# A two-network transformer kernel: the ALiBi bias from GpSimd to VectorE, and the norms' steps at other places among the products

## The chip, the cores and the metric

The kernel runs on one core of a Trainium2 chip. The metric is device time in microseconds (us) of one execution, from the first to the last instruction on the device, together with the little that lies around them. A kernel is run several times and the median counts.

## The reference, cut to what matters

Two networks run one after the other on 256 positions of 1024 features, in float32. The first has two layers, each an attention, a SwiGLU feed-forward and a gated input (PLE); the second has a convolution and pooling mixer, a feed-forward with a short convolution, an attention, and another such feed-forward.

```python
for i in range(DEPTH):                       # first network, two layers
    hn = rmsnorm(h, norm_mix[i])
    mix = diff_attention(hn, ...) if i % 2 == 0 else neighborhood_attention(hn, ...)
    h = h + mix
    h = h + swiglu(rmsnorm(h, norm_ffn[i]), ffn_w_gate[i], ffn_w_up[i], ffn_w_down[i])
    gate = jax.nn.sigmoid(rmsnorm(h, norm_ple[i]) @ ple_w_gate[i])
    h = h + gate * (p[i] @ ple_w_proj[i])
return rmsnorm(h, norm_final)
# second network: h += even_mixer(norm(h)); h += conv_ffn(norm(h))
#                 h += odd_mixer(norm(h));  h += conv_ffn(norm(h)); final norm
# in diff_attention, for each of 8 heads:
    dist = jnp.abs(qpos[:, None] - kpos[None, :]).astype(jnp.float32)
    bias = -slopes[:, None, None] * dist
    s = einsum('mbhqd,mbhkd->mbhqk', qblk, k) * scale + bias
# rmsnorm: x * rsqrt(mean(x * x) + eps) * g, a mean over the 1024 features
```

## The kernel before

Activations lie feature by feature: 8 tiles of 128 features (partitions) by 256 positions, handled as 4 banks of two tiles. The weights are streamed from HBM in chunks of 128 x 1024 by DMAs that SyncE issues, into a stage of 5 buffers. Each chunk is split into a rounded high part (`w_hi`, ScalarE, L96) and the rest (`w_lo`, VectorE, L97), into a pool of 8 buffers. Every product is done as three matmuls of a 128 x 128 weight with 256 columns (`mm3`, all at L220): high with high, high with low, low with high. The activations are split in the same manner (`u_hi` on ScalarE, L282, `u_lo` on VectorE, L284).

The order of the matmuls is written out by hand. The program counts steps: after every 12 matmuls (4 `mm3`) `tick()` moves a clock on and runs what is due, so `at(delay, f)` puts f among the products that follow, and splits of later chunks are paid out there too. The order on the other engines comes out of the order of emission through a scheduler.

A norm is folded into the products: they use `u`, the activations with the gain alone, and the results are multiplied by `R`, the factors 1/rms laid out over all partitions, when they are read from PSUM (the accumulator memory of TensorE). The factors take two steps, which `rstd_soon(n, a, b)` puts at two ticks. Step a (`rstd_a`) adds up the squares on TensorE (`ps_ss`, a matmul with ones that reads `half`, the VectorE sum at L291), scales on VectorE (L306), and takes the power on GpSimd (POOL, L307). Step b (`rstd_b`) spreads the result with two transposes on TensorE (`ps_r`, L323) and a copy on ScalarE (`R`, L325). `first_pairs(u, late=2)` lets four column tiles of weights (96 matmuls) start over the first 6 of the 8 feature tiles and takes the last 2, whose bank comes last, afterwards.

In an attention `qkv_group` computes q and k of a group (`ps_g`, 48 matmuls each), reads them with the factors, and then v (`ps_v`, 48 matmuls); the scores (`ps_S`) and the softmax run at ticks that the table `AT` lists. In the first group a loop waits with reading until R is emitted:

```python
while g == 0 and not hasattr(n, "R"):
    tick()
```

At the start of the program, SP loads x and the weights; GpSimd makes `dist` (the distances, 128 x 512) and, in `small_constants` at tick 9, multiplies it by the slopes of 8 heads: eight `tensor_scalar` of 128 x 512 (L573, `bias`). The same GpSimd queue holds the power of the first norm behind them. In PLE the four banks of the gate's products are read and turned into the new h in the order 0, 1 (both after the product of bank 2), 2, 3. In the feed-forwards a pair is 48 matmuls; the first two pairs come from `first_pairs`, and a product of the result (`acc`, reading `m` of L805) begins after the fourth.

Of the kernel before, what the change touches and what calls it, by code (L numbers as in the profile page):

```python
# [13 lines left out]
OP = mybir.AluOpType  # L14
# [19 lines left out]


AT = {
    "da": {"scores": (3, 9), "then": (6, 8, 12), "last": ((2, 5), (5, 7, 10)), 0: (6, 10)},
    "na": {"scores": (3, 9), "then": (6, 8), "last": ((2, 5), (5, 7)), 0: (6, 10)},
    "od": {"scores": (3, 9), "then": (6, 8), "last": ((2, 5), (5, 7)), 0: (12, 15), 1: (6, 9)},
}  # L40


# [81 lines left out]
def network(ctx: ExitStack, tc: tile.TileContext, x_t, p_t, cols, b_v, na_bias, t5_bias, w_mats, out):  # L124
# [88 lines left out]
    causal = off  # L213
    tri = const.tile([128, 128], F32, name="tri")

    def col(name, i):
        return ct[:, COL[name] + i:COL[name] + i + 1]

# [13 lines left out]
    def at(delay, f):  # L232
        clock[1] += 1
        due.append((clock[0] + delay, clock[1], f))
# [96 lines left out]
    def release():  # L331
        W.hold = False

    def rstd_soon(n, a=7, b=9):
        at(4, release)
        at(a, lambda: rstd_a(n))
        at(b, lambda: rstd_b(n))

    def bc2(r):
        return r[:, None, :].to_broadcast([128, 2, S])  # L340
# [127 lines left out]
    def qkv_group(n, g, kind, bv, steps):  # L468
        q = work.tile([128, 2, S], F32, tag="q", bufs=1, name="q")
        k = work.tile([128, 2, S], F32, tag="k", bufs=1, name="k")  # L470

        def parts(x, tag):
            hi = work.tile([128, 2, S], F32R, tag=tag + "h", name=tag + "_hi")
            lo = work.tile([128, 2, S], F32R, tag=tag + "l", name=tag + "_lo")
            nc.scalar.activation(hi, x, AF.Copy)
            nc.vector.tensor_sub(lo, x, hi.bitcast(F32))
            return x, hi, lo

        v = work.tile([128, 2, S], F32, tag="v", name="v")
        u = n.u  # L480
        ps_k = None
        if g == 0 and kind != "da":
            ps, ps_k = first_pairs(u)
        else:
            ps = pair(u)
            if g == 0:
                ps_k = pair(u)
        while g == 0 and not hasattr(n, "R"):
            tick()
        if kind == "na":  # L490
            t = work.tile([128, 2, S], F32, tag="qb", bufs=1, name="qb")
            nc.vector.tensor_mul(t, ps, bc2(n.R))
            for i in range(2):
                nc.scalar.activation(q[:, i, :], t[:, i, :], AF.Identity, bias=b_q8[:, 2 * g + i:2 * g + i + 1],
                                     scale=0.125)
        else:
            nc.vector.scalar_tensor_tensor(q, ps, 0.125, bc2(n.R), op0=OP.mult, op1=OP.mult)
        q = parts(q, "q")
        ps = ps_k or pair(u)
        if kind == "na":  # L500
            t = work.tile([128, 2, S], F32, tag="qb", bufs=1, name="kb")
            nc.vector.tensor_mul(t, ps, bc2(n.R))
            for i in range(2):
                nc.scalar.activation(k[:, i, :], t[:, i, :], AF.Identity, bias=col("b_k", 2 * g + i), scale=1.0)
        else:
            nc.vector.tensor_mul(k, ps, bc2(n.R))
        k = parts(k, "k")
        steps(q, k, v)
        if kind == "od" and g == 0:
            z = small.tile([128, 2, 8], F32, tag="zf", bufs=1, name="zf")  # L510
            pz = [psum.tile([128, 264], F32, tag=f"acc{2 + t}", name="pz") for t in range(2)]
            kk = 0
            for n_k in (3, 3, 2):
                hi, lo = W.take(n_k * 264)
                for i in range(n_k):
                    for t in range(2):
                        for a, b in ((0, hi), (1, hi), (0, lo)):
                            mm(pz[t], u[a][:, kk, t * 128:(t + 1) * 128], b[:, i * 264:(i + 1) * 264],
                               kk == 0 and (a, b) == (0, hi), kk == 7 and b is lo)
                    kk += 1  # L520
                    if kk % 2 == 0:
                        tick()
            for t in range(2):
                nc.scalar.activation(v[:, t, :], pz[t][:, :256], AF.Copy, scale=n.rstd[:, t:t + 1])
                nc.vector.scalar_tensor_tensor(z[:, t, :], pz[t][:, 256:264], n.rstd[:, t:t + 1],
                                               ct[:, COL["b_f"]:COL["b_f"] + 8], op0=OP.mult, op1=OP.add)
            fox_prepare(z, extra)
            return
        pv = psum.tile([128, 2, S], F32, tag="acc3", name="ps_v")
        for half in range(2):  # L530
            hi, lo = W.take(1024)
            for i in range(4):
                kk = 4 * half + i
                for t in range(2):
                    for c, (a, b) in enumerate(((0, hi), (1, hi), (0, lo))):
                        mm(pv[:, t, :], u[a][:, kk, t * 128:(t + 1) * 128], b[:, i * 256:(i + 1) * 256],
                           kk == 0 and t == 0 and c == 0, kk == 7 and c == 2, skip_group_check=True)
                if i % 2 == 1:
                    tick()
        for t in range(2):  # L540
# [26 lines left out]
    g_fm = const.tile([128, 8], F32, name="g_fm")  # L567

    def small_constants():

        nc.vector.scalar_tensor_tensor(dist, dist, -1.0, dist, op0=OP.mult, op1=OP.max)
        for hd in range(8):
            nc.gpsimd.tensor_scalar(da_tiles[hd // 4][:, hd % 4], dist, -2.0 ** (-8.0 * (hd + 1) / 8), None, op0=OP.mult)  # L573
        nc.vector.tensor_scalar(tri, off[:, :128], 0.0, None, op0=OP.is_ge)
        for g, w in enumerate(POOL_WINDOWS):
            nc.vector.tensor_scalar(rcnt[:, g, :], rcnt[:, g, :], float(w), None, op0=OP.min)
        nc.vector.reciprocal(rcnt, rcnt)
# [12 lines left out]
        nc.vector.tensor_mul(g_fm, ct[:, COL["norm_final"]:COL["norm_final"] + 8], ct[:, COL["mix2"]:COL["mix2"] + 8])  # L590
# [104 lines left out]
    def attention(n, kind, gain_next):  # L695
# [35 lines left out]
        nn, done = next_norm(gain_next)  # L731
        acc.last([(o[0][:, j, :], o[1][:, j, :]) for j in range(8 - N_LAST_ATT, 8)], 8 - N_LAST_ATT, done)
        assert not due
        rstd_soon(nn)
        return nn


# [121 lines left out]
    def ple(n, l, gain_next, after, final=False):  # L859
# [14 lines left out]
        for b in range(4):  # L874
            if b == 0:
                pgs = first_pairs(n.u, between=proj)
                held = [(i, pps[i], pgs[i]) for i in range(2)]
            elif b > 1:
                proj(b)
                held.append((b, pps[b], pair(n.u, *(("m", 2) if b == 2 else ("g", 2)))))  # L880
            if b < 2:
                continue
            for i, pp, pg in held:
                z = work.tile([128, 2, S], F32, tag="a", bufs=3, name="z")
                nc.vector.tensor_mul(z, pg, bc2(n.R))
# [13 lines left out]

    n = Norm()  # L900
    W.split(4, lambda b: norm_bank(n, b, h[:, 2 * b:2 * b + 2, :], lambda t: col("norm_mix", t)))
    W.split()
    for b in range(4):
        stats_bank(n, b, h[:, 2 * b:2 * b + 2, :])
        W.split()
    for _ in range(N_HI - 8):
        W.split()
    at(9, small_constants)
    ug = [const.tile([128, 2 + S], F32, name=f"ug{i}") for i in range(3)]
    for t in ug:  # L910
        nc.gpsimd.memset(t[:, 0:2], 0.0)
# [2 lines left out]
    for l in range(2):  # L914
        n = attention(n, ("da", "na")[l], lambda t, l=l: col("norm_ffn", 8 * l + t))
        n = ffn(n, swiglu_mid, lambda t, l=l: col("norm_ple", 8 * l + t))
        rstd_soon(n)
        if l == 0:
            def after(nn):
                rstd_soon(nn)  # L920
# [11 lines left out]
            nc.vector.scalar_tensor_tensor(h[:, t, :], h[:, t, :], col("norm_final", t), r,  # L932
                                           op0=OP.mult, op1=OP.mult)

    rstd_soon(n)
    at(8, scale_h)


    y = split_act()
# [64 lines left out]
    plan = [(pool_out, 0), (pool_out, 2), (gc_val, 0), (gc_val, 1), (gate_b, 0), (gc_val, 2), (gc_val, 3), (gate_b, 2)]  # L1004
    for i, (f, a) in enumerate(plan):
        if i == 0:
            first = first_pairs(n.u, tags[:2])
        ps = first[i] if i < 2 else pair(n.u, tags[i], 2 if tags[i] == "g" else 1)
        waiting.append((f, ps, a))
        if hasattr(n, "R"):  # L1010
# [13 lines left out]
    nn, done = next_norm(lambda t: col("ffn2", t))  # L1024
    acc.last([y_k(2), y_k(3)], 6, done)
    n = nn
    rstd_soon(n)
    load_t5()
    n = ffn(n, conv_mid(0), lambda t: col("mix2", 8 + t))
    rstd_soon(n)  # L1030
# [178 lines left out]
```

## Time and profile before

| | |
|---|---|
| Median of 3 runs | 1254.99 us (1249.63 to 1255.4) |
| The profiled execution: its own time | 1255.7 us |
| Its span, first to last instruction | 1253.9 us |
| Mean granted TensorE clock | 0.991 |
| TensorE busy (PE) | 1219.8 us, 97% |
| VectorE busy (DVE) | 930.2 us, 74% |
| ScalarE busy (ACT) | 693.4 us, 55% |
| GpSimd busy (POOL) | 56.5 us, 5% |
| SyncE's weight queue | 50.2% of the 16 DMA engines' span |

The page gives each engine's busy time as a share of the span. In rows of the timeline the first number is the start in us from the start of the span, the second the time to the end of the instruction (or of several alike, then with xN), and in brackets stands how long the engine idled before it and what ended that. A matmul overlaps the next, so its step is the distance of two starts.

### The profile page before, as it was taken

The page shows a single profiled execution, that of the slowest core. Times are in us where ns is not written, and L with a number is a line of the kernel's source. Part 1 is how long each engine was busy: PE and PEld are TensorE (multiplying, and loading weights), DVE is VectorE, ACT ScalarE, POOL GpSimd, SP SyncE. Part 2 cuts the span into 40 slices and gives each one's busy share as a digit, 9 for nine tenths or more (in the row PEclk, how much of TensorE's full clock was granted, in tenths as well). Part 3 has the DMA queues.
Part 4 walks back from the last instruction along what each step waited for, and adds up shares of the span by engine and source line. Part 5 has one row for each costly group of instructions (what it writes and reads, how often), then busy time and mean ns, then how long its engine had stood idle before and what let it go on. Part 6 is the DMA issues. An engine that isn't in the chain of part 4 may idle for free.

```text
span 1253.9 us, 25715 instructions
## 1 busy us (share of the span) xinstructions
PE 1219.8 (97%) x10448; PEld 1199.9 (96%) x10448; DVE 930.2 (74%) x1700; ACT 693.4 (55%) x1178; POOL 56.5 (5%) x64
## 2 busy tenths in 40 slices
PE   4999999999999999999999999999999999999997
PEld 4999999999999899999998999999999899999996
DVE  5876766666888767666678978777787876977773
ACT  4776644444667655454457555555455665545543
POOL 6011000000001000000000000000000000000000
PEclk9999999999999999999999999999999999999998
DMA  7554556555557436555544465555545333655530
GB/s 265 186 169 152 174 202 203 196 194 168 202 174 204 175 135 211 193 202 195 180 157 160 160 227 183 200 188 186 185 154 203 122 131 135 218 185 185 187 117 35
DMA packets 62935, 222.46 MB, mean 177 GB/s; under 512 B 7264, under 2 KB 7776, under 8 KB 62688
## 3 DMA queue, kind: packets, MB, share of 16 engines
q1 hardware_dynamic: 60768, 214.52, 50.2%
q0 software_dynamic: 1616, 5.77, 1.9%
q8 instruction: 82, 1.34, 0.4%
q10 hardware_dynamic: 432, 0.53, 0.1%
q14 instruction: 37, 0.30, 0.1%
HBM read 219.74 MB, written 1.05 MB: 176 GB/s over the span
## 4 chain that ended last, share of the span: by engine, by line
PE 86%; DVE 6%; issue 3%; POOL 2%; ACT 2%; DMA 1%; POOLq 0%; DVEq 0%; ACTq 0%; SPq 0%
PE ps_g L220 50%; PE acc L220 26%; PE ps_v L220 4%; DVE w_lo L97 2%; PE ps_V L220 2%; POOL bias L573 1%; PE ps_S L220 1%; PE ps_t L433 1%; POOL rstd L307 1%; ACT w_hi L96 1%; PE ps_p L220 1%; ACT sc L463 0%; PE pz L220 0%; DMA stage<-w_ev_out 0%; PE ps_ss L220 0%
## 5 line engine op out<-in xcount | busy, mean ns | idle before, releaser
L96 ACT ACTIVATE w_hi<-stage 128x1024 fp32r<-128x1024 f32 (+2 forms) x413 | 426.6, 1040 | 411.4 <-PE ps_g L220 174.4
L97 DVE TENSOR_TENSOR w_lo<-stage,w_hi 128x1024 fp32r<-128x1024 f32 (+2 forms) x413 | 493.1, 1201 | 194.8 <-ACT w_hi L96 191.3
L220 PE MATMUL ps_g<-u_hi,w_hi 128*128 128x256 f32 x2048 | 576.5, 281 | 10.2 <-ACT w_hi L96 7.0
L220 PE MATMUL ps_g<-u_hi,w_lo 128*128 128x256 f32 x2048 | 571.1, 279 | 1.2 <-DVE w_lo L97 1.2
L220 PE MATMUL ps_g<-u_lo,w_hi 128*128 128x256 f32 x2048 | 571.3, 279 | 0.7 <-DVE u_lo L284 0.6
L220 PEld LDWEIGHTS ps_g<-u_hi,w_hi 128*128 128x128 f32 x2048 | 386.2, 189 | 14.5 <-ACT w_hi L96 7.0
L220 PEld LDWEIGHTS ps_g<-u_hi,w_lo 128*128 128x128 f32 x2048 | 386.3, 189 | 1.4 <-DVE w_lo L97 1.4
L220 PEld LDWEIGHTS ps_g<-u_lo,w_hi 128*128 128x128 f32 x2048 | 385.8, 188 | 1.1 <-DVE u_lo L284 1.1
L220 PE MATMUL acc<-m,w_hi 128*128 128x256 f32 x1408 | 246.5, 278 | 0.1
L220 PEld LDWEIGHTS acc<-m,w_hi 128*128 128x128 f32 x1408 | 213.6, 188 | 0.4 <-DVE m L805 0.3
L220 PE MATMUL acc<-m,w_lo 128*128 128x256 f32 x704 | 195.4, 278 | 0.0
L220 PEld LDWEIGHTS acc<-m,w_lo 128*128 128x128 f32 x704 | 132.2, 188 | 0.0
L220 PE MATMUL acc<-u_hi,w_hi 128*128 128x256 f32 x256 | 73.0, 285 | 0.0
L220 PE MATMUL acc<-u_hi,w_lo 128*128 128x256 f32 x256 | 71.4, 279 | 0.0
L220 PE MATMUL acc<-u_lo,w_hi 128*128 128x256 f32 x256 | 71.3, 279 | 0.0
L463 ACT ACTIVATE sc<-sc,st 128x256 f32<-128x256 f32 (+1 forms) x96 | 46.0, 481 | 31.4 <-DVE st L461 31.3
L307 POOL TENSOR_TENSOR rstd<-rstd,mhalf 128x2 f32<-128x2 f32 x11 | 15.7, 1426 | 1036.6 <-DVE rstd L306 1036.6
L220 PE MATMUL ps_v<-w_hi,u_hi 128*128 128x256 f32 x176 | 52.5, 298 | 0.0
L220 PE MATMUL ps_v<-w_hi,u_lo 128*128 128x256 f32 x176 | 50.3, 286 | 0.0
L220 PE MATMUL ps_v<-w_lo,u_hi 128*128 128x256 f32 x176 | 50.3, 286 | 0.0
L220 PEld LDWEIGHTS acc<-u_hi,w_hi 128*128 128x128 f32 x256 | 48.0, 188 | 1.5 <-issue 1.1
L220 PEld LDWEIGHTS acc<-u_hi,w_lo 128*128 128x128 f32 x256 | 48.1, 188 | 0.0
(191 smaller groups left out, 1226.8 us busy)
## 6 DMA issues: line engine op xcount, KB each, us to landing
stage<-w_gu SPq DMA_DIRECT2D x88, 512.0 KB, 4.2
stage<-w_in SPq DMA_DIRECT2D x88, 512.0 KB, 4.2
stage<-w_down SPq DMA_DIRECT2D x44, 512.0 KB, 4.3
stage<-w_out SPq DMA_DIRECT2D x44, 512.0 KB, 4.3
stage<-w_na_qkv SPq DMA_DIRECT2D x24, 512.0 KB, 4.2
stage<-w_da_qkv SPq DMA_DIRECT2D x23, 512.0 KB, 4.3
stage<-w_od_in SPq DMA_DIRECT2D x22, 512.0 KB, 3.5
stage<-w_gate SPq DMA_DIRECT2D x16, 512.0 KB, 3.2
```

The source lines that it names most:

```text
L96: self.nc.scalar.activation(hi[:, s], t[:, s], AF.Copy)
L97: self.nc.vector.tensor_sub(lo[:, s], t[:, s], hi[:, s].bitcast(F32))
L220: nc.tensor.matmul(o, a, b, start=start, stop=stop, **kw)
L307: nc.gpsimd.tensor_tensor(n.rstd, st[:, 2:4], mhalf, op=OP.pow)
L433: nc.tensor.transpose(ps[:, o:o + 128], a[:, qt, kk * 128:(kk + 1) * 128], ident)
L463: nc.scalar.activation(sc[:, i, :widths[i]], sc[:, i, :widths[i]], AF.Exp, bias=st[:, 2 + i:3 + i], accum_out=st[:, 4 + i:5 + i])
L573: nc.gpsimd.tensor_scalar(da_tiles[hd // 4][:, hd % 4], dist, -2.0 ** (-8.0 * (hd + 1) / 8), None, op0=OP.mult)
```

## The change

- The eight ALiBi products go to VectorE. Three of them, with the small constants `tri`, `dist` and `rcnt`, are emitted at the start of the program, one at tick 9, four at tick 22.
- In `qkv_group` the loop that waited for R goes. In a first group q and k stay in PSUM, the v products follow at once, and `read()` between them reads q and k as soon as R is there. `AT` lets the first group's scores start a tick earlier (od: two).
- `rstd_soon` puts step b at tick 10 instead of 9; in the conv feed-forwards the steps are at 8 and 11 instead of 7 and 9, ahead of PLE at 5 and 7, ahead of the even mixer at 7 and 11, with `scale_h` (the rescaling of h there) at 13 instead of 8. The neighbourhood attention (na) and the even mixer (ev) take the last 4 feature tiles late instead of 2.
- PLE handles banks 0 and 1 right behind the first pairs.
- The second weight chunk is split in two halves.

```diff
-    "da": {..., 0: (6, 10)},
+    "da": {..., 0: (5, 9)},
...
+    def da_bias(heads):
+
+        for hd in heads:
+            nc.vector.tensor_scalar(da_tiles[hd // 4][:, hd % 4], dist, -2.0 ** (-8.0 * (hd + 1) / 8), None, op0=OP.mult)
+
+    nc.vector.tensor_scalar(tri, off[:, :128], 0.0, None, op0=OP.is_ge)
+    nc.vector.scalar_tensor_tensor(dist, dist, -1.0, dist, op0=OP.mult, op1=OP.max)
+    da_bias(range(3))
...
-    def rstd_soon(n, a=7, b=9):
+    def rstd_soon(n, a=7, b=10):
...
-        while g == 0 and not hasattr(n, "R"):
-            tick()
...
+        waiting = []
+        if g:
+            qs = evict_q(pair(u))
+            steps(qs, evict_k(pair(u)), v)
         else:
-            nc.vector.tensor_mul(k, ps, bc2(n.R))
-        k = parts(k, "k")
-        steps(q, k, v)
+            waiting += first_pairs(u, late=4 if kind == "na" else 2) if kind != "da" else [pair(u), pair(u)]
+
+        def read():
+            if waiting and hasattr(n, "R"):
+                qs = evict_q(waiting[0])
+                steps(qs, evict_k(waiting[1]), v)
+                waiting.clear()
...
                 if i % 2 == 1:
                     tick()
+                    read()
...
-        for hd in range(8):
-            nc.gpsimd.tensor_scalar(da_tiles[hd // 4][:, hd % 4], dist, -2.0 ** (-8.0 * (hd + 1) / 8), None, op0=OP.mult)
+        da_bias([3])
...
-        rstd_soon(nn)
+        rstd_soon(nn, *((8, 11) if kind == "od" else (7, 10)))
...
                 pgs = first_pairs(n.u, between=proj)
+                continue
+            if b == 1:
                 held = [(i, pps[i], pgs[i]) for i in range(2)]
-            elif b > 1:
+            else:
                 proj(b)
                 held.append((b, pps[b], pair(n.u, *(("m", 2) if b == 2 else ("g", 2)))))
-            if b < 2:
-                continue
...
-    W.split()
+    W.split(2)
...
+    at(22, lambda: da_bias(range(4, 8)))
...
-        rstd_soon(n)
+        rstd_soon(n, 5, 7)
...
-    rstd_soon(n)
-    at(8, scale_h)
+    rstd_soon(n, 7, 11)
+    at(13, scale_h)
...
-            first = first_pairs(n.u, tags[:2])
+            first = first_pairs(n.u, tags[:2], late=4)
...
-    rstd_soon(n)
+    rstd_soon(n, 8, 11)
```

VectorE at the start of the program, up to `half`, which the first sums of squares read. Before, from the small constants on (`dist`, `tri`, `rcnt`):

```order
L571 SCALAR_TENSOR_TENSOR dist<-dist 128x512
L574 TENSOR_SCALAR tri<-off 128x128
L576 TENSOR_SCALAR rcnt<-rcnt 128x16 x4
L97 TENSOR_TENSOR w_lo<-stage,w_hi 128x1024
L275 TENSOR_TENSOR ssq<-ssq,sq 128x512
L97 TENSOR_TENSOR w_lo<-stage,w_hi 128x1024 x2
L275 TENSOR_TENSOR ssq<-ssq,sq 128x512
L97 TENSOR_TENSOR w_lo<-stage,w_hi 128x1024
L275 TENSOR_TENSOR ssq<-ssq,sq 128x512
L577 RECIPROCAL rcnt<-rcnt 128x64
L97 TENSOR_TENSOR w_lo<-stage,w_hi 128x1024
L291 TENSOR_TENSOR half<-ssq 128x256
```

And of the change, from the first three bias instructions on:

```order
L219 TENSOR_SCALAR bias<-dist 128x512 x3
L225 TENSOR_SCALAR rcnt<-rcnt 128x16 x2
L296 SCALAR_TENSOR_TENSOR u_lo<-h,ct,u_hi 128x256
L226 RECIPROCAL rcnt<-rcnt 128x64
L296 SCALAR_TENSOR_TENSOR u_lo<-h,ct,u_hi 128x256
L97 TENSOR_TENSOR w_lo<-stage,w_hi 128x256
L97 TENSOR_TENSOR w_lo<-stage,w_hi 128x512 x2
L97 TENSOR_TENSOR w_lo<-stage,w_hi 128x1024
L287 TENSOR_TENSOR ssq<-ssq,sq 128x512
L97 TENSOR_TENSOR w_lo<-stage,w_hi 128x1024
L287 TENSOR_TENSOR ssq<-ssq,sq 128x512
L97 TENSOR_TENSOR w_lo<-stage,w_hi 128x1024 x2
```

Then come an `ssq`, two more `w_lo` of 128 x 1024, and `half`. Ahead of `half` there now stand three bias instructions and seven whole chunks (one of them in halves) instead of five.

TensorE at the start, around the two transposes `ps_r` that spread the first factors. Before, they stand ahead of all v products:

```order
L220 MATMUL ps_g<-u_hi,w_hi 128x256
L220 MATMUL ps_g<-u_lo,w_hi 128x256
L220 MATMUL ps_g<-u_hi,w_lo 128x256
L323 MATMUL ps_r<-ident,rstd 128x128 x2
L220 MATMUL ps_v<-w_hi,u_hi 128x256
L220 MATMUL ps_v<-w_hi,u_lo 128x256
```

And of the change, amid them:

```order
L232 MATMUL ps_v<-w_hi,u_hi 128x256
L232 MATMUL ps_v<-w_hi,u_lo 128x256
L232 MATMUL ps_v<-w_lo,u_hi 128x256
L335 MATMUL ps_r<-ident,rstd 128x128 x2
L232 MATMUL ps_v<-w_hi,u_hi 128x256
L232 MATMUL ps_v<-w_hi,u_lo 128x256
```

From the sums `ps_ss` to `ps_r` there were 12 matmuls (all `ps_g`); now there are 36 (12 `ps_g`, 24 `ps_v`), and 24 of v follow.

VectorE in the neighbourhood attention's first group, from the scaling of the sums to the first scores' `k_lo` (`qb` and `kb` are q and k read from PSUM, `v` waits for the last v product). Before:

```order
L306 TENSOR_SCALAR rstd<-ps_ss 128x2
L97 TENSOR_TENSOR w_lo<-stage,w_hi 128x1024 x2
L492 TENSOR_TENSOR qb<-ps_g,R 128x512
L97 TENSOR_TENSOR w_lo<-stage,w_hi 128x1024
L502 TENSOR_TENSOR kb<-ps_g,R 128x512
L476 TENSOR_TENSOR q_lo<-q,q_hi 128x512
L97 TENSOR_TENSOR w_lo<-stage,w_hi 128x1024 x2
L476 TENSOR_TENSOR k_lo<-k,k_hi 128x512
L542 SCALAR_TENSOR_TENSOR v<-ps_v,rstd,bv 128x256 x2
```

And of the change:

```order
L318 TENSOR_SCALAR rstd<-ps_ss 128x2
L97 TENSOR_TENSOR w_lo<-stage,w_hi 128x1024 x3
L496 TENSOR_TENSOR qb<-ps_g,R 128x512
L564 SCALAR_TENSOR_TENSOR v<-ps_v,rstd,bv 128x256 x2
L507 TENSOR_TENSOR kb<-ps_g,R 128x512
L97 TENSOR_TENSOR w_lo<-stage,w_hi 128x1024
L488 TENSOR_TENSOR q_lo<-q,q_hi 128x512
L97 TENSOR_TENSOR w_lo<-stage,w_hi 128x1024
L488 TENSOR_TENSOR k_lo<-k,k_hi 128x512
```

The two instructions on v, which need the last v product, now stand ahead of `kb`. The order of SyncE's loads is the same in both programs; GpSimd loses the eight bias instructions and keeps the rest in order. In the conv feed-forwards TensorE's order from the start of the first pair goes from 84 products, sums, 24 products, transposes, 84 products to 96, sums, 36, transposes, 60; ahead of PLE the sums come 24 matmuls earlier.

## Rows read from the trace of the kernel before

**Rows 1.** The page: busy time of each engine, and the chain by engine.
```profile
PE 1219.8 (97%) x10448; PEld 1199.9 (96%) x10448; DVE 930.2 (74%) x1700; ACT 693.4 (55%) x1178; POOL 56.5 (5%) x64
...
PE 86%; DVE 6%; issue 3%; POOL 2%; ACT 2%; DMA 1%; POOLq 0%; DVEq 0%; ACTq 0%; SPq 0%
```
**Rows 2.** TensorE's waits by what ended them: total us, times, longest us.
```profile
PE ps_r L323 <- POOL rstd L307: 9.0, 4, 7.6
PE ps_g L220 <- ACT u_hi L282: 2.5, 2, 1.9
```
**Rows 3.** Timeline of GpSimd at the start: start us, us, instruction.
```profile
11.73 18.50 POOL L573 TENSOR_SCALAR bias<-dist 128x512 f32<-128x512 f32 x8 [8.93 <-DVE dist L571]
30.20 0.73 POOL L307 TENSOR_TENSOR rstd<-rstd,mhalf 128x2 f32<-128x2 f32 x1
```
**Rows 4.** Timeline of TensorE at the start, and the chain's piece of v.
```profile
21.31 0.58 PE L220 MATMUL ps_ss<-ones,half 128*128 128x1 f32 x4 [0.51 <-DVE half L291]
...
30.98 0.69 PE L323 MATMUL ps_r<-ident,rstd 128*128 128x128 f32 x2 [7.57 <-POOL rstd L307]
31.66 7.40 PE ps_v L220 x48
```
**Rows 5.** Timeline of VectorE at the start.
```profile
10.95 0.68 DVE L571 SCALAR_TENSOR_TENSOR dist<-dist 128x512 f32<-128x512 f32 x1
11.55 0.22 DVE L574 TENSOR_SCALAR tri<-off 128x128 f32<-128x128 f32 x1
...
14.17 2.35 DVE L97 TENSOR_TENSOR w_lo<-stage,w_hi 128x1024 fp32r<-128x1024 f32 x2
...
20.34 0.83 DVE L291 TENSOR_TENSOR half<-ssq 128x256 f32<-128x256 f32 x1
21.09 0.28 DVE L578 TENSOR_SCALAR off<-off 128x256 f32<-128x256 f32 x1
```
**Rows 6.** Windows: length, busy us (count) of each engine, granted TensorE clock, DMA.
```profile
10.00:20.00 10.00, 8.84 (x68) 8.64 (x67) 10.00 (x18) 8.59 (x12) 8.27 (x2) 1.00 0.92 346
...
30.00:35.00 5.00, 4.02 (x19) 4.03 (x20) 2.63 (x3) 3.30 (x6) 0.92 (x2) 0.50 0.01 2
```
**Rows 7.** Timeline from PLE to the neighbourhood attention, TensorE.
```profile
347.52 0.39 PE L220 MATMUL ps_g<-u_hi,w_hi 128*128 128x256 f32 x1 [0.66 <-ACT u_hi L282]
359.10 0.43 PE L323 MATMUL ps_r<-ident,rstd 128*128 128x128 f32 x2 [0.52 <-POOL rstd L307]
```
**Rows 8.** Timeline from PLE to the even mixer, TensorE and VectorE, and a window there.
```profile
675.54 0.38 PE L220 MATMUL ps_g<-u_hi,w_hi 128*128 128x256 f32 x1 [1.87 <-ACT u_hi L282]
676.53 0.38 PE L220 MATMUL ps_g<-u_lo,w_hi 128*128 128x256 f32 x1 [0.61 <-DVE u_lo L284]
...
689.56 0.43 PE L323 MATMUL ps_r<-ident,rstd 128*128 128x128 f32 x2 [0.52 <-POOL rstd L307]
...
692.58 0.40 PE L323 MATMUL ps_r<-ident,rstd 128*128 128x128 f32 x2 [1.17 <-DVE rstd L314]
...
680.99 0.88 DVE L284 SCALAR_TENSOR_TENSOR u_lo<-h,g_fm,u_hi 128x256 fp32r<-128x256 f32 x2 [0.34 <-ACT u_hi L282]
...
660.00:680.00 20.00, 17.53 (x141) 17.13 (x140) 20.00 (x30) 14.80 (x26) 0.00 (x0) 0.93 0.60 213
```
**Rows 9.** Timeline at the odd attention's start, and in the second conv feed-forward.
```profile
950.43 0.43 PE L323 MATMUL ps_r<-ident,rstd 128*128 128x128 f32 x2 [0.42 <-POOL rstd L307]
...
1077.00 0.76 DVE L805 TENSOR_TENSOR m<-t,m 128x256 fp32r<-128x256 f32 x2
...
1077.45 0.41 PE L220 MATMUL acc<-m,w_hi 128*128 128x256 f32 x2
```
**Rows 10.** The chain: matmuls of the first SwiGLU feed-forward, then of a conv feed-forward.
```profile
136.80 9.89 PE ps_g L220 x84
150.19 9.53 PE ps_g L220 x84
...
779.42 11.31 PE ps_g L220 x96
```

More of the change, by code (lines that the diff above doesn't have):

```diff
@@ L36 @@
 AT = {
-    "da": {"scores": (3, 9), "then": (6, 8, 12), "last": ((2, 5), (5, 7, 10)), 0: (6, 10)},
-    "na": {"scores": (3, 9), "then": (6, 8), "last": ((2, 5), (5, 7)), 0: (6, 10)},
-    "od": {"scores": (3, 9), "then": (6, 8), "last": ((2, 5), (5, 7)), 0: (12, 15), 1: (6, 9)},
+    "da": {"scores": (3, 9), "then": (6, 8, 12), "last": ((2, 5), (5, 7, 10)), 0: (5, 9)},
+    "na": {"scores": (3, 9), "then": (6, 8), "last": ((2, 5), (5, 7)), 0: (5, 9)},
+    "od": {"scores": (3, 9), "then": (6, 8), "last": ((2, 5), (5, 7)), 0: (10, 13), 1: (6, 9)},
 }
@@ L214, in network @@
     tri = const.tile([128, 128], F32, name="tri")
+    def da_bias(heads):
[4 more added lines that the diff above has]
+    da_bias(range(3))
+    for g, w in enumerate(POOL_WINDOWS):
+        nc.vector.tensor_scalar(rcnt[:, g, :], rcnt[:, g, :], float(w), None, op0=OP.min)
+    nc.vector.reciprocal(rcnt, rcnt)
     def col(name, i):
@@ L480, in qkv_group @@
         u = n.u
-        ps_k = None
-        if g == 0 and kind != "da":
-            ps, ps_k = first_pairs(u)
-        else:
-            ps = pair(u)
-            if g == 0:
-                ps_k = pair(u)
-        while g == 0 and not hasattr(n, "R"):
-            tick()
[L490 to L505, printed above, removed]
-            nc.vector.tensor_mul(k, ps, bc2(n.R))
-        k = parts(k, "k")
-        steps(q, k, v)
+        def evict_q(ps):
+            if kind == "na":
+                t = work.tile([128, 2, S], F32, tag="qb", bufs=1, name="qb")
+                nc.vector.tensor_mul(t, ps, bc2(n.R))
+                for i in range(2):
+                    nc.scalar.activation(q[:, i, :], t[:, i, :], AF.Identity, bias=b_q8[:, 2 * g + i:2 * g + i + 1],
+                                         scale=0.125)
+            else:
+                nc.vector.scalar_tensor_tensor(q, ps, 0.125, bc2(n.R), op0=OP.mult, op1=OP.mult)
+            return parts(q, "q")
@@ new lines, in evict_k @@
+        def evict_k(ps):
+            if kind == "na":
+                t = work.tile([128, 2, S], F32, tag="qb", bufs=1, name="kb")
+                nc.vector.tensor_mul(t, ps, bc2(n.R))
+                for i in range(2):
+                    nc.scalar.activation(k[:, i, :], t[:, i, :], AF.Identity, bias=col("b_k", 2 * g + i), scale=1.0)
+            else:
+                nc.vector.tensor_mul(k, ps, bc2(n.R))
+            return parts(k, "k")
+        waiting = []
+        if g:
+            qs = evict_q(pair(u))
+            steps(qs, evict_k(pair(u)), v)
+        else:
+            waiting += first_pairs(u, late=4 if kind == "na" else 2) if kind != "da" else [pair(u), pair(u)]
@@ L522, in qkv_group @@
                         tick()
+                        read()
+            assert not waiting
             for t in range(2):
@@ L539, in qkv_group @@
                     tick()
+                    read()
+        assert not waiting
         for t in range(2):
@@ L569, in small_constants @@
     def small_constants():
-        nc.vector.scalar_tensor_tensor(dist, dist, -1.0, dist, op0=OP.mult, op1=OP.max)
-        for hd in range(8):
-            nc.gpsimd.tensor_scalar(da_tiles[hd // 4][:, hd % 4], dist, -2.0 ** (-8.0 * (hd + 1) / 8), None, op0=OP.mult)
[L574 to L577, printed above, removed]
+        da_bias([3])
         nc.vector.tensor_scalar(causal, off, 128.0, NEG, op0=OP.is_gt, op1=OP.mult)
@@ L876, in ple @@
                 pgs = first_pairs(n.u, between=proj)
+                continue
+            if b == 1:
                 held = [(i, pps[i], pgs[i]) for i in range(2)]
-            elif b > 1:
+            else:
                 proj(b)
                 held.append((b, pps[b], pair(n.u, *(("m", 2) if b == 2 else ("g", 2)))))
-            if b < 2:
-                continue
             for i, pp, pg in held:
```

## The prediction

> **What bounds the kernel now.** I read the page first. TensorE is busy 97% of the span, VectorE 74%, GpSimd 5%, and the chain that ended last is TensorE for 86% [rows 1]. So only two things can give time back: stretches in which TensorE stands still, and stretches in which its matmuls go slower than they could. The list of TensorE's waits comes next: the largest entry that this change touches is the transposes `ps_r` waiting for GpSimd's power, 9.0 us in four waits, 7.6 of them in one; then the products waiting for a late `u_hi`, 2.5 us in two [rows 2]. The span less TensorE's busy time is 1253.9 - 1219.8 = 34 us, all that waits could give. Then I read the timeline around each of them.
>
> The big one is at the start. GpSimd works off the eight bias instructions from 11.73 for 18.50 us, and the power of the first norm, queued behind them, starts at 30.20 [rows 3]. TensorE has the sums at 21.31, needs them back 12 matmuls later and waits 7.57 us, to 30.98; the 48 v products behind it end at 31.66 + 7.40 = 39.06 [rows 4]. The wait costs a second time: from 30 to 35 the granted clock is 0.50, its lower level (1.2 GHz), and TensorE had been idle before [rows 6]. At the full step of 9.53/84 = 0.1135 us [rows 10] 48 products take 5.4 us, not 7.4: 2.0 us are lost to the clock.
>
> **The start of the program.** Eight instructions leave GpSimd. They took 18.50/8 = 2.31 us each [rows 3]; without them only the power is left in that queue, and it is done 0.73 us after VectorE has scaled the sums. The price moves to VectorE. No row shows this instruction there, but neighbours do: one input, one scalar, 128 x 256 takes 0.28 us and 128 x 128 takes 0.22; a two-input instruction of 128 x 512 takes 0.68 [rows 5]. The first two give a slope of 0.06 per 128 columns, so about 0.40 for 512; the bounds are 0.28 and 0.68. I take 0.40, since the form is that of the first two rows.
>
> On VectorE this isn't free, since it was busy 10.00 of 10.00 us from 10 to 20 [rows 6], and `half`, which the sums read, now stands behind three bias instructions and two more weight chunks (a chunk is 2.35/2 = 1.18 us). `half` started at 20.34 [rows 5]; it now starts near 20.34 + 3 x 0.40 + 2 x 1.18 = 23.9, and the sums near 24.8, where they stood at 21.31. So the wait of 0.51 us at the sums [rows 4] grows to about 4.0. From the sums to the transposes there were 30.98 - 21.31 - 7.57 = 2.1 us of work; now 24 v products (2.7 us) are added, so the transposes come at 29.6. The power is done near 26.3, well ahead: no wait. After 0.7 for the transposes and 2.7 for the other 24 v products, v ends at 33.0 instead of 39.06: 6.1 us. A wait of 4.0 us may bring the low clock too, as 7.57 did for 2.0 us; I take half of that, 1.0, which leaves 5.1. The five other bias instructions (2.0 us) fall in 25 to 45, where VectorE had idled for want of the factors (busy 2.63 of 5.00 us from 30 to 35 [rows 6]); I cost them at nothing, and if that cover is gone (weight chunks late behind them) it is up to 1. **Start: -5.0** (from -3.3, with 0.68 per bias and the whole 2.0 of the clock, to -9.6, if `half` is not delayed at all: 7.57 + 2.0).
>
> A rule speaks against this part. The Trainium skill, GPSIMD Engine Reference, section 4.1 Engine selection, has elementwise work of one input run at roughly line-rate on GpSimd. By that rule eight instructions at VectorE's price would end long before the sums, and moving them would bring nothing; the trace disagrees, with 2.31 us each and the wait of 7.57.
>
> **From PLE to the neighbourhood attention: 0.** Two waits stand there, 0.66 for bank 2 of u and 0.52 for the power [rows 7]. With four tiles taken late, the first is reached 36 matmuls later and goes; with 36 instead of 12 matmuls between sums and transposes so does the second. But bank 3 is needed earlier (after 54 matmuls, not 72), and VectorE's order puts two instructions that need the last v product ahead of `kb`, so `k_lo` comes some 0.8 us late for the scores. Bounds -1.5 to +1.5.
>
> **From PLE to the even mixer: -2.2.** TensorE waits 1.87 and 0.61 us for bank 2, then 0.52 and 1.17 at the two pairs of transposes [rows 8], 4.2 in all. The late four and the wider distance remove these. What is late next is bank 3, whose `u_lo` starts at 680.99 on a VectorE that is busy 20.00 of 20.00 us from 660 to 680 [rows 8]. Bank 2's first matmul at 675.54 is the thirteenth of the mixer, so the mixer begins near 675.54 - 1.87 - 12 x 0.1135 = 672.3, and 54 matmuls on, at 678.4, it will want bank 3. Banks 0 and 1 are handled earlier, so I put bank 3 at about 680.4 and the new wait at 2.0 us. Bounds: 0.5 left of the gain if bank 3 doesn't come forward (a wait of 3.5), 5 if it comes in time and the low clock that the 0.93 of that window shows goes too. `scale_h` is put off, which keeps VectorE free for the reads; it comes back later while TensorE runs on 20 us of products.
>
> **Odd attention: -0.4**, the wait at its transposes [rows 9], with 24 matmuls more in between.
>
> **Conv feed-forwards: +0.6.** Sums go one step later and the factors two. In the second one `m` is being written (1077.00 for 0.76 us, two of them) just as the first `acc` matmul starts at 1077.45 [rows 9]: no slack. The factors come 24 matmuls (2.8 us) later; VectorE had spent much of that on weight chunks, so most is hidden, and I take 0.6 (0 to 2.0 for the two). The SwiGLU feed-forwards get their factors 12 matmuls later; there no wait for `m` stands in the list, and the change delays it by 12 x 0.1135 = 1.4 us, a quarter of a pair's 48 matmuls: 0, and up to 1 each if that cover is gone.
>
> **The halves of chunk 2** and the other tick shifts: 0; they move no instruction past another that TensorE waits for, except those counted.
>
> **Sum:** 5.0 + 0 + 2.2 + 0.4 - 0.6 = 7.0 us. The profiled execution took 1255.7 us, so the sum gives 1248.7; it lies 0.7 above the median of 1255.0, from which it gives 1248.0. I predict **1248.0 us**.
>
> **Rivals.**
>
> *All of it comes back.* If the scheduler's order on VectorE doesn't bind (`half` and bank 3 arrive as early as before), the start gives 9.6, the mixer 5, the neighbourhood attention 1.2, the odd attention 0.4, the feed-forwards cost nothing: 16 us, 1239. For it speaks that VectorE idles right behind the start [rows 6]; against it that this hole lies behind `half`, and that VectorE is full ahead of both places.
>
> *Waits replace waits; no change.* `half` comes 4 us later and brings the whole low-clock spell (gain 3.3), bank 3 costs the mixer most of its gain (0.5 left), the neighbourhood attention loses 1.5 to `kb` and `k_lo`, and the feed-forwards 2.0: net 0 to 1, 1254 to 1255. For it speaks VectorE's 10.00 of 10.00 and 20.00 of 20.00 in both stretches; against it that each of these is at its bad end.
>
> *Slower, by the step of the matmuls.* In the first SwiGLU feed-forward 84 matmuls take 9.89 us ahead of the factors' transposes and 9.53 behind them (0.1177 and 0.1135 each); in a conv feed-forward, 96 take 11.31, 0.1178, behind the transposes too [rows 10], at a granted clock of 1.00 in both. I found no cause. The change moves these transposes by 12 to 24 matmuls. A feed-forward has 22 x (48 + 24) = 1584 matmuls, some 1450 of them behind the transposes; if both SwiGLU ones stay at the longer step, that is 2 x 1450 x 0.0043 = 12.5 us, which gives 1260.5, and with the feed-forwards' 2.0 the kernel is at 1262, slower than before by over 0.5%. It decides from both on; one alone gives 1254. The opposite can happen: a conv feed-forward that falls into the short step gives 6 us more.
>
> **Chances.** The forecast (a net of 4 to 10 us) 0.5; all of it, or a step that falls the right way, 0.18; no change through new waits or one feed-forward at the longer step 0.24; slower 0.08. A measurement of this kernel can hardly tell less than 0.5%, 6.3 us, from no change, so the border of faster is at 1248.7 and that of slower at 1261.3. Of the forecast's 0.5, about 0.32 lies below 1248.7. Faster 0.32 + 0.18 = 0.5, same 0.18 + 0.24 = 0.42, slower 0.08. The range for 8 in 10 runs from 1239.5 (all of it) to 1255.5 (new waits eat it); it leaves the slower case out, and the upper end of the gain.
>
> **What would show it.** In the profile of the changed kernel: no wait of `ps_r` for the power above 1 us; a wait at the first `ps_ss` for `half` of about 4 us; v's end near 33; bias on VectorE near 0.40 each. At the mixer, no wait for bank 2 and one of about 2 us for bank 3, none at the transposes. At the conv feed-forwards an `acc` that waits for `m` by under 1 us. The step of the matmuls behind the transposes of each feed-forward: 10.88 or 11.31 per 96. I am wrong if `half` is not late at all (then the gain is near twice as large), if TensorE finds another wait right behind the start (weights that arrive late now that the products come 6 us sooner), or if a feed-forward changes its step.

## The result and the profile after

The change made the kernel slower: 1261.86 us median of 8 runs (1257.39 to 1265.85) against 1255.49 (1249.63 to 1256.32), a ratio of 1.0062 with a 95% interval of 1.0043 to 1.0082. The 8 runs lie in two groups, four from 1257.4 to 1259.5 and four from 1264.2 to 1265.9. The profiled execution took 1259.39 us, 3.7 above that of before.

The page after the change, the row of busy times:

```profile
PE 1228.1 (98%) x10448; PEld 1207.3 (96%) x10448; DVE 932.4 (74%) x1709; ACT 692.3 (55%) x1179; POOL 34.4 (3%) x56
```

And the longest of TensorE's waits that are new or changed (total, times, longest):

```profile
PE ps_g L232 <- ACT u_hi L294: 3.5, 2, 3.0
PE ps_g L232 <- DVE z_ev L988: 2.4, 1, 2.4
PE ps_ss L232 <- DVE half L303: 2.2, 2, 1.3
PE ps_S L232 <- DVE k_lo L488: 1.6, 3, 1.0
```

The wait for GpSimd's power (9.0 us before [rows 2]) is gone from the list, yet TensorE is busy 1228.1 us instead of 1219.8 [rows 1]: the same 10448 matmuls take longer. Where, is read from the distances between landmarks on TensorE's timeline (the first `acc` matmul of each stage, the first `ps_p` of each PLE, the first `ps_pool`). Worked out from their starts, in us:

| stretch | before | after | change |
|---|---|---|---|
| start to the first attention's output | 108.86 | 102.38 | -6.5 |
| to the first product of SwiGLU 1's result | 50.69 | 51.03 | +0.3 |
| SwiGLU 1 from there | 157.76 | 157.76 | 0 |
| PLE 1 and the neighbourhood attention | 117.28 | 118.58 | +1.3 |
| to the first product of SwiGLU 2's result | 51.77 | 52.15 | +0.4 |
| SwiGLU 2 from there | 157.75 | 163.95 | +6.2 |
| PLE 2 and the mixer (two stretches) | 83.61 | 86.44 | +2.8 |
| to the first product of conv 1's result | 45.89 | 46.08 | +0.2 |
| conv 1 and the odd attention | 253.11 | 252.47 | -0.6 |
| to conv 2's, and to TensorE's last row | 218.33 | 218.94 | +0.6 |

So the start gave 6.5 us; one feed-forward, whose matmuls have no wait at all in that stretch, took 6.2 back, and the mixer and the neighbourhood attention the rest. (The changes add up to +4.7; behind TensorE's last row the profile after is 1.0 us shorter, 7.8 instead of 8.9.)

**The start.** The timeline of VectorE, GpSimd and TensorE:

```profile
10.81 1.08 DVE L219 TENSOR_SCALAR bias<-dist 128x512 f32<-128x512 f32 x3
23.71 0.42 DVE L303 TENSOR_TENSOR half<-ssq 128x256 f32<-128x256 f32 x1
25.50 0.75 POOL L319 TENSOR_TENSOR rstd<-rstd,mhalf 128x2 f32<-128x2 f32 x1 [22.69 <-DVE rstd L318]
24.28 0.58 PE L232 MATMUL ps_ss<-ones,half 128*128 128x1 f32 x4 [1.34 <-DVE half L303]
30.52 0.38 PE L335 MATMUL ps_r<-ident,rstd 128*128 128x128 f32 x2
```

And the chain's piece behind the transposes:

```profile
30.90 2.75 PE ps_v L232 x24
```

A bias takes 1.08/3 = 0.36 us. The power is done 4.3 us ahead of the transposes, which wait for nothing; v ends at 33.65, where it ended at 39.06 [rows 4].

**The step of the matmuls.** The chain of the two SwiGLU feed-forwards, from behind the factors' transposes:

```profile
145.18 8.39 PE ps_g L232 x72
153.57 5.44 PE acc L232 x48
159.01 10.88 PE ps_g L232 x96
...
473.47 8.60 PE ps_g L232 x72
482.07 5.65 PE acc L232 x48
487.72 11.31 PE ps_g L232 x96
```

The first keeps the short step of before, 10.88 us per 96; the second goes at 11.31, as the conv ones do [rows 10]. What lies between the transposes and this, in the second one, on TensorE and VectorE:

```profile
475.80 0.28 PE L232 MATMUL ps_g<-u_lo,w_hi 128*128 128x256 f32 x1
475.92 0.28 PE L232 MATMUL ps_g<-u_hi,w_lo 128*128 128x256 f32 x1
476.14 0.39 PE L232 MATMUL ps_g<-u_hi,w_hi 128*128 128x256 f32 x1
476.37 0.28 PE L232 MATMUL ps_g<-u_lo,w_hi 128*128 128x256 f32 x1
...
474.26 1.23 DVE L97 TENSOR_TENSOR w_lo<-stage,w_hi 128x1024 fp32r<-128x1024 f32 x1 [0.61 <-ACT w_hi L96]
475.40 1.28 DVE L850 TENSOR_TENSOR gu<-ps_g,R 128x512 f32<-128x512 f32 x2
```

The fourth pair's first matmul starts 0.22 us after its neighbour instead of 0.11, and so does the one behind it, 0.23: a stall too small for the list. The pair needs the PSUM bank of an earlier pair, which VectorE reads (`gu`) as soon as R is there. R now comes 12 matmuls later, and a chunk's `w_lo` stands ahead of the read, so the first read ends near 476.0. Up to there the step is 0.113; behind it 0.118, to the end of the feed-forward.

The first SwiGLU feed-forward has the same stall at the same place, and its step doesn't change:

```profile
147.63 0.28 PE L232 MATMUL ps_g<-u_hi,w_lo 128*128 128x256 f32 x1
147.86 0.38 PE L232 MATMUL ps_g<-u_hi,w_hi 128*128 128x256 f32 x1
148.08 0.28 PE L232 MATMUL ps_g<-u_lo,w_hi 128*128 128x256 f32 x1
```

So the stall alone doesn't say which step follows; the experiments count how often it is the longer one.

**The mixer.** TensorE's waits and two of VectorE's rows there:

```profile
683.49 0.39 PE L232 MATMUL ps_g<-u_hi,w_hi 128*128 128x256 f32 x1 [3.01 <-ACT u_hi L294]
690.36 0.61 PE L232 MATMUL ps_ss<-ones,half 128*128 128x1 f32 x4 [0.88 <-DVE half L303]
725.18 0.58 PE L232 MATMUL ps_g<-u_hi,w_hi 128*128 128x256 f32 x1 [2.42 <-DVE z_ev L988]
...
708.54 2.85 DVE L948 SCALAR_TENSOR_TENSOR h<-h,ct,R 128x256 f32<-128x256 f32 x7
724.44 0.68 DVE L988 TENSOR_TENSOR z_ev<-ps_g,R 128x512 f32<-128x512 f32 x1
```

Three waits of 6.3 us stand where there were five of 4.9 [rows 8 and the 0.70 for z_ev that the list of before had]. The postponed rescaling (L948, eight instructions) now falls amid the mixer's reads.

### The profile page after: what moved, and what is told of

It reads as the page before. It is cut to its first block, busy times and chain, and to the rows that moved or that the text cites. A ratio compares the mean times of both kernels' runs of the same rounds, so it can differ in the third digit from the quotient of the medians.

```text
span 1257.6 us, 25726 instructions
## 1 busy us (share of the span) xinstructions
PE 1228.1 (98%) x10448; PEld 1207.3 (96%) x10448; DVE 932.4 (74%) x1709; ACT 692.3 (55%) x1179; POOL 34.4 (3%) x56
## 3 DMA queue, kind: packets, MB, share of 16 engines
q8 instruction: 82, 1.34, 0.4%
## 4 chain that ended last, share of the span: by engine, by line
PE 83%; DVE 10%; ACT 3%; issue 2%; DMA 1%; POOL 0%; POOLq 0%; DVEq 0%; ACTq 0%; SPq 0%
PE ps_g L232 48%; PE acc L232 26%; DVE w_lo L97 4%; PE ps_v L232 3%; ACT w_hi L96 1%; PE ps_V L232 1%; PE ps_S L232 1%; PE ps_t L445 1%; ACT sc L475 1%; DVE u_lo L296 1%; DVE sc L471 1%; PE pz L232 0%; PE ps_p L232 0%; DMA stage<-w_da_qkv 0%; PE ps_ss L232 0%
## 5 line engine op out<-in xcount | busy, mean ns | idle before, releaser
L232 PE MATMUL acc<-m,w_hi 128*128 128x256 f32 x1408 | 249.1, 279 | 0.3 <-DVE m L820 0.2
L232 PEld LDWEIGHTS acc<-u_lo,w_hi 128*128 128x128 f32 x256 | 48.1, 188 | 0.0
```

The lines of the kernel that those rows point to most:

```text
L232: nc.tensor.matmul(o, a, b, start=start, stop=stop, **kw)
```

## The experiments

Three theories of the step stood at the beginning: the wait (a short wait behind the transposes lets TensorE go on in the longer step), the place (it is where the transposes stand), and chance.

**e1: factors of the SwiGLU feed-forwards back to tick 9.**

```diff
-        rstd_soon(nn, *((8, 11) if kind == "od" else (7, 10)))
+        rstd_soon(nn, *((8, 11) if kind == "od" else (7, 9)))
```

> The changed kernel, with the factors ahead of the two SwiGLU feed-forwards at tick 9 again (10 in the change). Theory 1, the wait: the fourth pair's wait of 0.22 us for its bank, which came with the later factors, lets TensorE go on in its longer step. Then there is no such wait here, both SwiGLU feed-forwards run 96 matmuls in 10.88 us, and the time is near 1259.4 - 5.8 = 1253 in most runs. Theory 2, the place: it is where the transposes stand that sets the step; it expects the same here as theory 1. Theory 3, chance: the step is taken by chance in each execution and the change has no part in it; then times spread as those of the change, 1257 to 1266.

1247.54 us (1243.48 to 1252.19, 12 runs), ratio to before 0.995 (0.9929 to 0.9972). With one tick in two places the median is 14 us below that of the change. In its profile (1246.13) both SwiGLU feed-forwards are short, and the second conv one too, which this edit doesn't touch. The 12 runs lie in two groups of six, 1243.5 to 1246.1 and 1248.9 to 1252.2, which fits that conv feed-forward being short in half of them; so not all of the 14 us are the tick's. From the first SwiGLU feed-forward:

```profile
143.32 9.53 PE ps_g L232 x84
152.84 5.44 PE acc L232 x48
158.28 10.88 PE ps_g L232 x96
```

**e2: the kernel before with that one tick.**

```diff
-        rstd_soon(nn)
+        rstd_soon(nn, 7, 9 if kind == "od" else 10)
```

> The kernel before, with this one part of the change: factors ahead of the two SwiGLU feed-forwards at tick 10. Theories 1 and 2: the fourth pair waits some 0.2 us, one or both SwiGLU feed-forwards run at 11.31 us per 96, and the median is 5 to 12 us above before, 1260 to 1268. Theory 3: as before, within 1 us.

1268.75 us (1261.81 to 1270.72), ratio 1.011 (1.0081 to 1.0139), with both SwiGLU feed-forwards long (the profiled run, 1261.81, is the fastest of the six; its first conv feed-forward is short):

```profile
150.52 8.60 PE ps_g L220 x72
159.12 5.65 PE acc L220 x48
164.77 11.31 PE ps_g L220 x96
```

The 24 matmuls right behind the transposes go at 0.113; then come the two doubled steps at the fourth pair, then 0.118. Chance as the whole cause falls; the wait and the place remain.

**e3: a later read in the kernel before, the transposes unmoved.**

```diff
         gu = work.tile([128, 2, S], F32, tag="a", bufs=3, name="gu")
+        if j == 0:
+            for _ in range(2):
+                nc.vector.tensor_mul(gu, h[:, 0:2, :], bc2(R))
```

> The kernel before, with two more VectorE products of 128 x 512 ahead of the first read of a SwiGLU feed-forward's result (their output is overwritten). The transposes stay where they were, and the fourth pair should wait about 1.0 us for its bank. Theory 1, the wait: steps of 11.31 per 96 in one or both SwiGLU feed-forwards in most runs, 1261 to 1269. Theory 2, the place: 10.88 as before, 1257. Theory 3: as before plus the two waits, 1257.

1253.71 us, 0.9994 (0.9977 to 1.001), both short. It tells nothing of the theories: VectorE read another pair first, at 151.95, and the fourth pair didn't wait. It shows only that two more VectorE instructions without a wait cost nothing.

**e5: the same ahead of the first two reads.**

```diff
+        if j < 2:
+            for _ in range((2, 2)[j]):
+                nc.vector.tensor_mul(gu, h[:, 0:2, :], bc2(R))
```

> The kernel before, with two more VectorE products of 128 x 512 ahead of each of the first two reads of a SwiGLU feed-forward (their output is overwritten), four in all, so that no bank is read before the fourth pair needs one; the transposes stay where they were. The fourth pair should now wait some 0.6 us (the lighter version of this had left no wait). Theory 1, the wait: the short step right behind the transposes turns into the longer one at this wait, in one or both SwiGLU feed-forwards in most runs; median 1260 to 1269. Theory 2, the place of the transposes: both SwiGLU feed-forwards stay at 10.88 per 96, 1256.

1268.44 us (1268.11 to 1268.90), ratio 1.0104 (1.0091 to 1.0117). The wait in the first SwiGLU feed-forward, on TensorE's timeline:

```profile
154.75 0.39 PE L220 MATMUL ps_g<-u_hi,w_hi 128*128 128x256 f32 x1 [0.58 <-DVE gu L838]
```

And the chain from there:

```profile
154.75 5.92 PE ps_g L220 x48
160.68 5.65 PE acc L220 x48
166.33 11.31 PE ps_g L220 x96
```

With the transposes where they were, 0.58 us of waiting in each SwiGLU feed-forward cost 13 us, in all four runs. The wait is enough; the transposes needn't move.

**e4: two more transposes, behind all early waits of the changed kernel.**

```diff
+                if j == 5:
+                    extra_r = psum.tile([128, S], F32, tag="m", bufs=2, name="ps_x")
+                    for t in range(2):
+                        nc.tensor.transpose(extra_r[:, t * 128:(t + 1) * 128],
+                                            n.both[:, t:t + 1].to_broadcast([128, 128]), ident)
```

> The changed kernel with two more transposes on TensorE (into a bank that nobody reads) ahead of the sixth pair of each feed-forward, behind all its early waits. In every trace so far the factors' transposes in front of products without a wait left the short step. If transposes choose it, all four feed-forwards run 96 matmuls in 10.88 us from there, and the time is near 1259.4 - 5.8 - 2 x 6 = 1242. If the conv feed-forwards always go at the longer step, only the SwiGLU ones gain: 1253. If the step is chance, times spread from 1240 to 1266.

1253.96 us (1245.74 to 1259.18). The second expectation names 1253 too, but not for its reason. In the profile (1257.27) the extra pair turned one feed-forward of four short, the second SwiGLU one:

```profile
492.93 5.65 PE ps_g L232 x48
498.58 0.22 PE ps_x L833 x2
498.80 5.45 PE ps_g L232 x48
504.25 5.44 PE acc L232 x48
```

In the second conv feed-forward it did the opposite:

```profile
1085.89 5.44 PE ps_g L232 x48
1091.33 0.22 PE ps_x L833 x2
1091.55 5.65 PE ps_g L232 x48
```

In the other two the step stayed at 0.118. Transposes can bring the short step or end it. The expectation's premise, that transposes without a wait behind them had always left the short step, was wrong too: in the kernel before, the conv feed-forwards go at 0.118 right behind theirs.

**e7: the mixer's part undone in the changed kernel.**

```diff
-    rstd_soon(n, 7, 11)
-    at(13, scale_h)
+    rstd_soon(n, 7, 9)
+    at(8, scale_h)
...
-            first = first_pairs(n.u, tags[:2], late=4)
+            first = first_pairs(n.u, tags[:2])
```

> The changed kernel with the even mixer's part undone: factors at ticks 7 and 9, the rescaling of h at 8, two feature tiles late. If the late four and the late rescaling are what the mixer loses by, the wait for bank 3 (3.0 us), the one for the last sums (0.9) and the one for z (2.4) give way to those of before (1.9 and 0.6, 0.5 and 1.2, 0.7), and the start of the conv feed-forward behind it comes 3.3 us sooner against the end of PLE. If PLE's new order of banks is to blame, little of that comes back. Steps of the feed-forwards as in the change; time 1256, or 1261 to 1263 with no short SwiGLU feed-forward.

1262.48 us (1256.55 to 1264.35). PLE 2 and the mixer take 65.58 + 19.16 = 84.7 us, 1.7 less than after, not 3.3 less. The wait for z_ev falls from 2.4 to 0.5, so that one comes with this part; that it is the rescaling's, and not the ticks' or the late tiles', is argued from VectorE's rows and wasn't tried alone. The wait of the sums for `half` grows to 3.3.

**e9: the factors of all four feed-forwards back.** e1 with `rstd_soon(n, 7, 9)` ahead of the conv ones too.

> The changed kernel with the factors of all four feed-forwards at ticks 7 and 9 again. The SwiGLU ones as in the first run of this study (both short). The conv ones: if the later factors made them go short there (one of them did), they are long again and the time is 1250; if not, it stays at 1247.5.

1249.53 us (1248.79 to 1250.88), 0.995 (0.9937 to 0.9963): both SwiGLU short, both conv long, as expected.

**e8: only the start and the odd attention.** In the changed kernel all other places are written as before (na keeps its wait for R ahead of v, PLE its order, `late=2`, all factors at 9 but those two):

```diff
+    rstd_soon(n, 7, 10)                       # first norm, odd attention
...
+        while kind == "na" and waiting:
+            if not hasattr(n, "R"):
+                tick()
+            read()
```

> Of the change only the start (bias on VectorE, q and k read amid v, the halved chunk) and the odd attention's first group; the neighbourhood attention, the mixer, PLE and all four feed-forwards as before. The start gives 6.1 us and the odd attention 0.5, and the steps are those of before (both SwiGLU feed-forwards short, the conv ones long in most runs): 1255.2 - 6.6 = 1248.6; if the steps fall otherwise by chance, 6 us more or less for each feed-forward.

1245.41 us (1245.07 to 1247.63), ratio 0.9924 (0.9912 to 0.9935). Its start takes 99.99 us to the first attention's output, 8.9 less than before. That is 2.4 more than in the profile after, where the granted clock was 0.68 from 15 to 20 and 0.66 from 25 to 30; here it was 1.00 in both. The rest of its landmarks are those of before within 0.5 us. e8 and e9 differ only by PLE's order, the neighbourhood attention's part and the mixer's, with the feed-forwards' steps alike in their profiles: these three parts cost 4.1 us together (1249.53 against 1245.41).

**e10: e8 with the factors of all feed-forwards at 6 and 8.** The two calls that stand for them, behind the attentions and ahead of the first conv feed-forward, become `rstd_soon(nn, 6, 8)` and `rstd_soon(n, 6, 8)`.

> The kernel of e8 (start and odd attention of the change, the rest as before) with the factors of all four feed-forwards a tick sooner than before, at 6 and 8. No wait can come of that at the fourth pair. Theory 1, the wait: both SwiGLU feed-forwards stay short, 10.88 per 96; of the conv ones it says nothing: as in e8 both longer (1245.4), or 6 us less for each that turns short. Theory 2, the place: with the transposes 12 matmuls from where they were, on the other side, the SwiGLU ones go long, 1251 to 1258.

1239.73 us (1238.88 to 1245.77), ratio 0.9898 (0.9875 to 0.9922), the fastest version. The SwiGLU feed-forwards stay short, so the place falls in this direction. The runs lie in two groups, four from 1238.9 to 1239.9 and two from 1245.4 to 1245.8. In the profile (1239.61) the first conv feed-forward is short, where e8 has 11.31; whether the earlier factors bring that, or chance, isn't shown:

```profile
765.07 5.44 PE acc L232 x48
770.51 10.88 PE ps_g L232 x96
```

**e11, e12, e13: one part of the change each, on top of e8** (edits as in the change: the mixer's three places; PLE's order with its factors at 5 and 7; the neighbourhood attention's reading, `late=4`, factors at 10 and `AT`).

> The kernel of e8 with the mixer's part of the change (factors at 7 and 11, the rescaling of h at 13, four feature tiles late). From the first product of the second PLE to the first of the mixer's output e8 took 64.27 + 19.10 = 83.4 us and the change 86.4. If this part is what loses there, it takes some 85 to 86.5 here, 1247 to 1248.5; if my prediction's step holds by itself (waits of bank 2 and of the transposes gone, one of 2 us for bank 3), 81 to 82, 1243.

> The kernel of e8 with PLE's part of the change (banks 0 and 1 read right behind the first pairs, the factors ahead of PLE at 5 and 7). If its order of banks is what makes bank 3 late, the second PLE and the mixer take some 1 us more than the 83.4 of e8, and the first PLE with the neighbourhood attention up to 1 us more than 117.3; if it only brings reads forward, up to 1 us less in each: 1243.5 to 1247.5.

> The kernel of e8 with the neighbourhood attention's part of the change (q and k read amid v, four feature tiles late, factors at 10, the scores a tick sooner). If the new wait for k_lo (1.0 us) and the one for bank 3 are its work, the first PLE with this attention takes 1.2 us more than the 117.3 of e8, 1246.6; if my prediction's 0 holds, 1245.4.

| | median us | PLE 1 and na | PLE 2 and mixer |
|---|---|---|---|
| e8 | 1245.41 | 117.28 | 64.27 + 19.10 = 83.4 |
| e11, mixer | 1247.51 | 117.57 | 61.84 + 21.50 = 83.3 |
| e12, PLE | 1248.21 | 117.90 | 65.16 + 19.22 = 84.4 |
| e13, na | 1247.20 | 118.78 | 65.32 + 19.06 = 84.4 |

e11's own waits, u_hi, z_ev and `half`:

```profile
PE ps_g L232 <- ACT u_hi L294: 3.2, 2, 2.6
PE ps_g L232 <- DVE z_ev L993: 2.5, 1, 2.5
PE ps_ss L232 <- DVE half L303: 2.1, 2, 1.2
```

In these profiles the mixer's part alone shows neither the expected loss nor my gain of 2.2. It has the same long waits as after. Of the 3.1 us that after takes more, 2.4 are the matmuls' pace: after the waits of 3.01 and 2.42 us the profile of the change shows 13 and 12 steps of 0.21 us, that of e11 none (25 steps, 0.095 us each above 0.115). But e8 has such a spell too (17 steps, granted clock 0.83 in a window of 10 us), so 83.3 against 83.4 isn't like with like. In e2 and e5, which have the mixer of before and no spell there (granted clock 1.00 throughout), the stretch takes 82.7 and 82.1 us; against these the mixer's part costs about 1 us. e11's median, 2.1 us above e8, is where the expectation of a loss put it, but 1.8 of that lie at the start in its profile (101.80 us against 99.99), which the part doesn't touch.

In their profiles PLE's order costs 1.0 us at the mixer and 0.6 at the neighbourhood attention. The neighbourhood part costs 1.5, with the 1.0 us wait for `k_lo`; the 1.0 more that e13 has at the mixer, which it doesn't touch, is a longer spell of 0.21 us steps (granted clock 0.66 in a window of 10 us there, 0.83 in e8), so single stretches with waits are uncertain by 1 to 2 us. With all three parts the stretch of PLE 2 and the mixer took 86.4, 86.7, 86.1 and 84.6 us (after, e1, e9, e4).

## Why the prediction was wrong, step by step

The medians split the loss of 6.4 us: the start and the odd attention -10.0 (e8), the parts of PLE, the neighbourhood attention and the mixer +4.1 (e9 against e8), the later factors of the four feed-forwards +12.3 (the change against e9). The prediction had -5.4, -2.2 and +0.6 for these.

*The step that failed is the SwiGLU feed-forwards at 0.* I had costed the later factors by `m`, which has slack, and said that the delay of 12 matmuls was covered. The instruction that is late next is another: the read that frees the fourth pair's bank. The stall itself is 0.2 us, and 0 would have been nearly right for it. What it does to the matmuls behind it isn't: e2 and e5 show 13 to 14 us for two feed-forwards, e9 and e1 that it comes back with the tick. The profile of the change has one of them long; the two groups of its runs lie some 6 us apart, one feed-forward's price, which fits one and both long, but isn't shown: the profile is of a run in the lower group, and a conv feed-forward has the same price.

*The third rival* had the effect and its price (12.5 us for both; a stretch of 163.95 against 157.75 makes it 12.4) and the place in the program. But it had tied the step to where the transposes stand, without a cause, and gave it 8 in 100. That its 1262 is the median to 0.2 us is luck: it is added to a forecast of 1248 in which the start was too small and the mixer had the wrong sign. Of 14 feed-forwards in the profiles of after, e1, e2, e4, e5 and e7 where the short step behind the transposes met the fourth pair's wait, 12 went on in the longer one. Of 18 SwiGLU feed-forwards without that wait (before, e1, e3, e8 to e13), all 18 stayed short. So a wait there mostly ends the short step, and without one it was never lost; why two of 14 kept it stays open. The later place without a wait wasn't tried; the earlier one (e10) is harmless.

*The start, -5.0:* right, and rather low. Bias 0.36 (0.40 predicted), `half` at 23.71 (23.9), sums at 24.28 (24.8), v's end at 33.65 (33.0), no wait for the power; -6.5 in the profile after, -8.9 in e8, and between them in the eight other profiles with this start. One term was mis-sized: the wait for `half` is 1.34 us, not 4.0, since the products ahead of the sums end later too (the last starts at 22.66, in e8 at 22.07, before at 20.52). GpSimd's 2.31 us for an instruction that VectorE does in 0.36 is now measured on both sides, a factor of 6.4. The Trainium skill (GPSIMD Engine Reference, section 4.1 Engine selection) states that one-input work runs at roughly line-rate on GpSimd; these two numbers don't bear that out.

*The neighbourhood attention, 0:* +1.3, at the bad end of its bounds (+1.5), by the `k_lo` that I had named (1.0 us), with a share of PLE's order (e12).

*The mixer, -2.2:* +2.8. Bank 2's wait and the transposes' did go, but the waits rose by 1.4 us in all (6.3 against 4.9), and 25 steps of 0.21 us follow them where there were 17. Three terms failed: bank 3's wait was 3.0 instead of 2.0; the wait of the last sums for `half`, 0.9, wasn't in the sum; and the postponed rescaling was costed at nothing because TensorE had 20 us of products. It takes 3.3 us (0.47 + 2.85) of a VectorE that was full (10.00 of 10.00 us from 705.85 to 715.85), ahead of the z_ev for which TensorE then waits 2.4 instead of 0.7. e11, with this part alone and without a low-clock spell, shows no gain either.

*Odd attention, -0.4, and conv feed-forwards, +0.6:* -0.6 and +0.8, right.

## What to carry to other kernels

Before moving a norm's factors later, list every reader of R on the slower engine and every buffer that a read gives free; the first to run out need not be the one that the result waits for. Take each part of a bundle by itself: the start with the odd attention (e8) is a gain of 10 us, the whole a loss of 6. And a stall of 0.2 us, which a list of waits leaves out, is worth a look when a long run of matmuls follows it: compare the distance of starts ahead of it and behind.

## What the runs showed of the hardware that was not expected

At a granted clock of 1.00, the same matmuls of 128 x 256 run at one of two steps, 0.1133 or 0.1178 us, and can keep it over more than 1400 matmuls. In the 56 feed-forwards of the 14 profiles the step changes only at something irregular on TensorE, the transposes or a wait; at the sums of squares it changes in none. What in such a moment decides between the two stays open. The transposes of the factors were followed by the short step in all 28 SwiGLU feed-forwards, in 9 of the 14 first conv ones and in none of the 14 second ones. The extra transposes of e4 brought it once, ended it once and left the longer one twice. A wait mostly ended it, but in e1's second conv feed-forward a wait brought it.
